# A state space stage in a hybrid decoder: response matrices loaded without their zero corner, first ones at the end of the MLP before it, and its small products one weight tile later

## The chip, the cores and the metric

The kernel runs on one core of one Trainium2 chip. The metric is the device time of one execution in microseconds (us). "TensorE" is PE in the profile, "VectorE" DVE, "ScalarE" ACT, "GpSimd" POOL and "SyncE" SP; SP and POOL are the two engines that issue the DMAs named below.

## What is computed

Two layers over 256 tokens of width 2048, each a token mixer, a cross-attention to 256 memory tokens and a squared-ReLU MLP of width 8192, with RMSNorm before each and residual adds. The mixer of layer 0 is a chunked gMLP, that of layer 1 the state space layer that the change touches:

```python
def s5_glu(h, w_in, lam_re, lam_im, log_dt, bm_re, bm_im, cm_re, cm_im, d_skip, w_out, b_out):
    u = (h @ w_in).astype(F32).reshape(bsz, seq, B_GROUPS, B_GROUP)     # 128 groups of 16 channels
    lam_bar = jnp.exp(lam * dt)                                         # 64 complex states per group
    b_bar = ((lam_bar - 1.0) / lam)[..., None] * bmat
    bu = jnp.einsum('gpc,bsgc->sbgp', b_bar, u.astype(jnp.complex64))
    _, states = lax.associative_scan(combine, (a, bu), axis=0)          # s_t = lam_bar * s_(t-1) + bu_t
    y = jnp.einsum('gcp,sbgp->bsgc', cmat, states).real + d_skip.astype(F32) * u
    y = jax.nn.gelu(y.reshape(bsz, seq, B_WIDTH), approximate=False).astype(h.dtype)
    val, gate = jnp.split(y @ w_out + b_out, 2, axis=-1)
    return val * jax.nn.sigmoid(gate)
```

Everything is fp32 in and out.

## The kernel before

**Weights.** A weight matrix is read in tiles of 128x1024 fp32 (512 KB). `wload` (L123) issues a tile's DMA on SP into `wraw` (4 buffers); `wtile` has ACT cast it to its high part `whi` (L102) and DVE subtract that to get the low part `wlo` (L103), 3 buffers each. A product is three matmuls, whi with the activations' high part, wlo with their high part, whi with their low part, so a tile is 12 matmuls of 128x512. In the state space stage they stand at L154, in the MLP at L171/L173 (up) and L801 to L803 (down).

**Order of the work.** After each weight tile's matmuls the program calls `tick()`. A tick runs what `at(delay, fn)` planned for it, and in the first MLP every second tick takes one step from the list `side`. So delays count weight tiles, and each engine's instruction order is fixed by when the program writes them, except that a side step is written with a priority of 200 instructions later. `issue_after(self.fed)` holds a DMA on SP behind the last weight load written so far.

**Side steps in the first MLP (`ssm_prep`, 680 to 1320 us).** The matrices that the state space stage needs are worked out beside the first MLP's matmuls and stored to DRAM: `Pd` (inputs to states), `Qd` (states to outputs) and `Kd` (the response of 8 positions to their own inputs, a band of 15x16 values per group and channel). For each of 32 quads of groups there are three steps: `quad` loads (`lb<-in_b_pc` and `lb<-Ld`, L1047), `quad_q` makes `Qd` and `Kd` (matrix products at L1085, stores at L1081 and L1093), `quad_p` makes `Pd` (DVE L1103 to L1106, store L1107).

**The state space stage (`s5`).** `gemm_tok` multiplies by `b_w_in` in four column chunks n of 8 tiles each. After chunk n, `chunks(n)` scales and reorders the result into `u` (DVE L1161, ACT L1164), and `follow(n)` plans the small products by weight tiles: `inputs` (8 transposes of `u` on PE, L1175) at 3, `own` (products with `pq`, L1189) at 4, `states` (transposes L1205, copies to `vv` on ACT L1209, whose first column is zeroed by POOL, L1200) at 5, `carry` (the scan, four DVE operations L1221 to L1224 each) at 6 to 9, `outputs` (products with `dq` L1237 and `qq` L1243) in two halves at 13 and 15, `features` (gelu on ACT L1250, transposes on PE L1255, split into high and low part on ACT L102 and DVE L103) at 17. `dq` is read from the band in `Kd` as full 128x1024 matrices: of the band of 8 positions to 8, what lies ahead of the diagonal is zeros that `quad_q` stored.

**Loads of the small matrices.** `pq`, `dq` and `qq` have 4 buffers each and 4 loads of 512 KB per chunk. For chunk 0, `pq` is issued on POOL as soon as the last store is done, `dq` on SP among the weight loads (ticks 2, 6, 10, 14), and `qq` on POOL at ticks 6 and 8 after chunk 0. For chunks 1 to 3 all three go through POOL, `pq` at 4, `dq` and `qq` at 6 and 8.

**The GLU.** `b_w_out` follows in the same way. Its first three accumulators are fed by k-ranges so that late features are needed late: k-tiles 0 to 7 three times, then 8 to 11 three times, a `flush()` of the plan, and 12 to 15. Chunk n's features are k-tiles 4n to 4n+3.

Of the kernel before, what the change touches and what calls it, by code (L numbers as in the profile page):

```python
# [16 lines left out]
P = 128  # L17
# [21 lines left out]
class Trunk:  # L39
# [854 lines left out]
    def ssm_prep(self, pool):  # L894
# [220 lines left out]
        for q in range(G // 4):  # L1115
            sd += [lambda q=q: quad(q), lambda q=q: quad_q(q), lambda q=q: quad_p(q)]


    def s5(self, x, cur, nxt):
# [3 lines left out]
        with tc.tile_pool(name="s5", bufs=2, reuse_waits="tile") as sp:  # L1123
# [5 lines left out]
            def load(src, nm, shape, stream):  # L1129
                t = sp.tile(shape, F32, name=nm, bufs={"pq": 4, "dq": 4, "qq": 4}[nm])  # L1130
                if stream:
                    with tc.issue_after(self.fed):
                        nc.sync.dma_start(out=t, in_=src)
                else:
                    nc.gpsimd.dma_start(out=t, in_=src)
                return t

            def fetch(nm, n, i, stream=False):

                if nm == "pq":  # L1140
                    t = load(self.Pd[4 * n + i], nm, [P, 2, 4, P], stream)
                elif nm == "qq":
                    t = load(self.Qd[4 * n + i].rearrange("l p r n -> (l p) r n"), nm, [P, 2, 4 * P], stream)
                else:
                    kd = self.Kd[4 * n + i]
                    t = load(bass.AP(tensor=kd.tensor, offset=kd.offset,
                                     ap=[[P, T], [(2 * T - 1) * P, 16], [1, T * P]]), nm, [P, T * P], stream)
                ahead[nm, n, i] = t
# [46 lines left out]
            def states(n):  # L1195
# [4 lines left out]
                nc.gpsimd.memset(vv[:, :, 0, :], 0.0)  # L1200
# [45 lines left out]
            def features(n):  # L1246
                py = st.pop(n)[2]
                y = sp.tile([P, T, 4, 2, 16], F32, name="y", tag="z", bufs=1)
                for l in range(2):
                    nc.scalar.activation(out=y[:, :, :, l, :].rearrange("p j i c -> p i j c"),  # L1250
                                         in_=py[l].rearrange("p i (j c) -> p i j c", j=T), func=AF.Gelu)
                for h in range(2):
# [7 lines left out]
            def follow(n):  # L1260

                for i in range(4):
                    if n + 1 < NCH:
                        self.at(4, lambda i=i: fetch("pq", n + 1, i))
                    if n:
                        self.at(6 + i // 2 * 2, lambda i=i: fetch("dq", n, i))
                    self.at(6 + i // 2 * 2, lambda i=i: fetch("qq", n, i))
                self.at(3, lambda: inputs(n))
                self.at(4, lambda: own(n))
                self.at(5, lambda: states(n))  # L1270
                self.at(6, lambda: [carry(n, 2, 15), carry(n, 4, 7, 2)])
                self.at(7, lambda: [carry(n, c, 1, 4) for c in (8, 12, 16)])
                self.at(8, lambda: [carry(n, c, 1, 4) for c in (20, 24, 28)])
                self.at(9, lambda: [carry(n, 6, 7, 2), carry(n, 3, 15)])
                self.at(13, lambda: outputs(n, 0))
                self.at(15, lambda: outputs(n, 1))
                self.at(17, lambda: features(n))

            for i in range(4):
                fetch("pq", 0, i)  # L1280
                self.at(4 * i + 2, lambda i=i: fetch("dq", 0, i, True))
# [9 lines left out]
            for j in range(NCH):  # L1291
                if j == 0:
# [4 lines left out]
                    av, ag, _ = (part(n, acc, (0, 8)) for n, acc in ((0, None), (NCH, None), (1, av1)))  # L1297
                    for n, acc in ((0, av), (NCH, ag), (1, av1)):
                        part(n, acc, (8, 12))
# [210 lines left out]
```

## Time and profile before

| | us |
|---|---|
| median of 3 runs | 2824.2 |
| the runs | 2821.84, 2825.02, 2824.2 |
| the profiled execution's own time | 2824.95 |
| its span, first to last instruction | 2823.2 |
| outside the span | 1.75 |

The profiled execution stands 0.75 us above the median. In the profile each engine has its own row of work; a row of the waits names the engine that sat idle, the operation it sat before, and the operation whose end released it. PEclk is the granted TensorE clock as a share of full speed; its two levels are 1.2 and 2.4 GHz.

### The profile page before, as it was taken

Reading aid. Unit: us, or ns where it says so; the run is one execution under the profiler, and the core shown is the slowest. Engines: PE = TensorE matmul, PEld = TensorE weight load, DVE = VectorE, ACT = ScalarE, POOL = GpSimd, SP = SyncE. Lnnn points to the kernel's source line nnn. Section 1 sums busy time; section 2 is a strip of 40 time slices with the busy share of each in tenths; the row PEclk is TensorE's granted clock in tenths of the full one; section 3 lists DMA queues with packets and bytes.
Section 4 is the critical chain, followed back from the end, with each engine's and each line's share of the span. In section 5 each row is a group of like instructions: output and inputs, shape, how many; then the busy total and the mean of one; then the engine's idle time right before and its main releaser. Section 6 shows DMA issues by size and latency. Waiting matters only on the chain.

```text
span 2823.2 us, 39558 instructions
## 1 busy us (share of the span) xinstructions
PE 2781.1 (99%) x15020; PEld 2329.6 (83%) x15020; DVE 1993.0 (71%) x2743; ACT 1399.7 (50%) x1801; POOL 202.6 (7%) x378
## 2 busy tenths in 40 slices
PE   9999999999999999999989999999999999999998
PEld 7888888888888888888867888888888888888886
DVE  6755756788878878786557667557777767667665
ACT  6445545555434444344445445445554545445444
POOL 0100000001022222221001000000000000000000
PEclk9999999999999999999999999999999999999999
DMA  8767655548688888887679777564556566565655
GB/s 289 231 205 217 209 179 172 180 148 262 196 270 260 249 257 262 249 262 234 189 237 284 220 214 224 177 195 152 182 160 215 171 216 194 163 217 166 218 177 157
DMA packets 189615, 596.85 MB, mean 211 GB/s; under 512 B 37632, under 2 KB 39856, under 8 KB 188912
## 3 DMA queue, kind: packets, MB, share of 16 engines
q1 hardware_dynamic: 151936, 532.22, 60.6%
q0 software_dynamic: 37344, 62.04, 8.1%
q8 instruction: 117, 1.92, 0.3%
q14 instruction: 74, 0.61, 0.1%
q10 hardware_dynamic: 144, 0.07, 0.0%
HBM read 570.66 MB, written 23.46 MB: 210 GB/s over the span
## 4 chain that ended last, share of the span: by engine, by line
PE 88%; DVE 4%; issue 3%; DMA 2%; ACT 2%; POOL 0%; ACTq 0%; SPq 0%; POOLq 0%; DVEq 0%
PE acc L171 23%; PE acc L718 21%; PE acc L154 13%; PE acc L173 12%; PE acc L801 4%; PE acc L803 4%; PE acc L802 4%; DVE wlo L103 1%; DMA wraw<-in_b_w_in 1%; PE ps L503 1%; ACT whi L102 1%; PE ps L581 1%; PE ps L154 1%; PE ps L222 1%; ACT u L1164 0%
## 5 line engine op out<-in xcount | busy, mean ns | idle before, releaser
L103 DVE TENSOR_TENSOR wlo<-wraw,whi 128x1024 fp32r<-128x1024 f32 x892 | 1090.6, 1224 | 662.4 <-ACT whi L102 658.0
L102 ACT CAST whi<-wraw 128x1024 fp32r<-128x1024 f32 x892 | 938.2, 1053 | 1154.2 <-PE acc L171 385.1
L171 PE MATMUL acc<-act,whi 128*128 128x512 f32 x3072 | 1084.4, 397 | 0.0
L173 PE MATMUL acc<-act,wlo 128*128 128x256 f32 x3072 | 863.1, 281 | 1.2 <-DVE wlo L103 1.2
L171 PEld LDWEIGHTS acc<-act,whi 128*128 128x128 f32 x3072 | 576.5, 188 | 139.7 <-issue 3.4
L173 PEld LDWEIGHTS acc<-act,wlo 128*128 128x128 f32 x3072 | 580.3, 189 | 2.7 <-DVE wlo L103 2.0
L154 PE MATMUL acc<-whi,act 128*128 128x512 f32 x1472 | 464.6, 394 | 15.8 <-ACT whi L102 14.1
L154 PEld LDWEIGHTS acc<-whi,act 128*128 128x128 f32 x1472 | 278.2, 189 | 75.8 <-ACT whi L102 14.5
L154 PE MATMUL acc<-wlo,act 128*128 128x512 f32 x736 | 287.9, 392 | 4.0 <-DVE wlo L103 4.0
L718 PE MATMUL acc<-whi,act 128*128 128x512 f32 x864 | 273.6, 390 | 1.2 <-DVE ends L560 1.0
L802 PE MATMUL acc<-wlo,hh 128*128 128x512 f32 x544 | 212.1, 390 | 3.2 <-DVE wlo L103 3.2
L801 PE MATMUL acc<-whi,hh 128*128 128x512 f32 x544 | 213.5, 392 | 0.0
L803 PE MATMUL acc<-whi,hl 128*128 128x512 f32 x544 | 212.6, 391 | 0.0
L718 PEld LDWEIGHTS acc<-whi,act 128*128 128x128 f32 x864 | 162.0, 188 | 37.6 <-ACT whi L102 2.6
L718 PE MATMUL acc<-wlo,act 128*128 128x512 f32 x432 | 168.7, 390 | 0.0
L154 PEld LDWEIGHTS acc<-wlo,act 128*128 128x128 f32 x736 | 138.7, 188 | 33.3 <-DVE wlo L103 5.3
L718 PE MATMUL acc<-whi,hh 128*128 128x512 f32 x378 | 147.6, 394 | 0.5
L718 PE MATMUL acc<-wlo,hh 128*128 128x512 f32 x378 | 147.2, 389 | 0.0
L718 PE MATMUL acc<-whi,hl 128*128 128x512 f32 x378 | 146.1, 389 | 0.0
L802 PEld LDWEIGHTS acc<-wlo,hh 128*128 128x128 f32 x544 | 102.1, 188 | 24.4 <-DVE wlo L103 3.5
L801 PEld LDWEIGHTS acc<-whi,hh 128*128 128x128 f32 x544 | 102.1, 188 | 22.8 <-issue 2.0
L803 PEld LDWEIGHTS acc<-whi,hl 128*128 128x128 f32 x544 | 102.1, 188 | 22.3 <-issue 1.0
(364 smaller groups left out, 2674.0 us busy)
## 6 DMA issues: line engine op xcount, KB each, us to landing
wraw<-in_f_w_up SPq DMA_DIRECT2D x256, 512.0 KB, 4.4
wraw<-in_f_w_down SPq DMA_DIRECT2D x228, 512.0 KB, 4.3
wraw<-in_a_w_in SPq DMA_DIRECT2D x64, 512.0 KB, 4.7
wraw<-in_x_w_q SPq DMA_DIRECT2D x64, 512.0 KB, 3.7
wraw<-in_x_w_k SPq DMA_DIRECT2D x64, 512.0 KB, 3.6
wraw<-in_b_w_out SPq DMA_DIRECT2D x64, 512.0 KB, 4.6
wraw<-in_x_w_v SPq DMA_DIRECT2D x48, 512.0 KB, 4.4
wraw<-in_x_w_o SPq DMA_DIRECT2D x48, 512.0 KB, 4.1
```

Of the source, the lines that this page charges most:

```text
L102: self.nc.scalar.copy(out=hi, in_=src)
L103: return self.nc.vector.tensor_tensor(out=lo, in0=src, in1=hi.bitcast(F32), op=ALU.subtract).ins
L154: nc.tensor.matmul(out[t], pairs[m][0][:, kt, sl], pairs[m][1][:, kk, :], start=st and m == 0, stop=en and m == 2)
L171: nc.tensor.matmul(acc[:, f, :], hi[:, kk, sl], both[:, kt].rearrange("p a s -> p (a s)"), start=st, stop=False, skip_group_check=True)
L173: nc.tensor.matmul(acc[:, f, 0:S], lo[:, kk, sl], ah[:, kt, :], start=False, stop=en, skip_group_check=True)
L222: nc.tensor.transpose(pt[:, kk, t * P:(t + 1) * P], src[:, t, c:c + P], self.ident)
L503: mm = lambda s, m, b, e: nc.tensor.matmul(sc[:, t, :], s, m, start=b, stop=e, skip_group_check=True)
L581: mm = lambda s, mv, b, e: nc.tensor.matmul(op[:, k, :], s, mv, start=b, stop=e, skip_group_check=True)
L718: mm = lambda s, m, e: nc.tensor.matmul(out, s, m, start=key not in begun, stop=e, skip_group_check=True)
L801: nc.tensor.matmul(acc[:, t, :], ah[:, kt % 4, sl], hi[:, kk, :], start=st, stop=False)
L802: nc.tensor.matmul(acc[:, t, :], ah[:, kt % 4, sl], lo[:, kk, :], start=False, stop=False)
L803: nc.tensor.matmul(acc[:, t, :], al[:, kt % 4, sl], hi[:, kk, :], start=False, stop=en)
```

## The change

- In `ssm_prep` two empty side steps stand between the first `quad_q` and the first `quad_p`; all later side steps come 4 ticks later.
- The response matrices live in four fixed tiles whose zero corner is written once (12 memsets on POOL). Each is then loaded by four DMAs of 32 partitions, of 256, 512, 768 and 1024 values per partition, 320 KB together, in place of one of 512 KB.
- Chunk 0's `dq` are issued on POOL right behind its `pq`; chunk 0's `qq` on SP at ticks 2, 4, 6, 8.
- The zeroing of `vv`'s first column moves from POOL to DVE.
- In `follow` everything is one tile later (`own` is written ahead of the fetches of that tile), and `features` is cut in two: the gelu (`activated`) right after the second half of `outputs`, transposes and split at 19 for chunks 0 and 1, at 17 for chunks 2 and 3.
- The GLU's first parts are cut finer: k-tiles 0 to 3, 4 to 7 and 8 to 11, three accumulators each.

```diff
--- before.py
+++ after.py
@@ -1113,7 +1113,10 @@
         sd += [lambda k=k: power(k) for k in range(5, T + 1)]
         sd += [lambda: spread(5), lambda: (last(), inputs(0))]
         for q in range(G // 4):
-            sd += [lambda q=q: quad(q), lambda q=q: quad_q(q), lambda q=q: quad_p(q)]
+            sd += [lambda q=q: quad(q), lambda q=q: quad_q(q)]
+            if q == 0:
+                sd += [lambda: None] * 2
+            sd += [lambda q=q: quad_p(q)]
 
 
     def s5(self, x, cur, nxt):
@@ -1126,25 +1129,33 @@
 
             ahead = {}
 
-            def load(src, nm, shape, stream):
-                t = sp.tile(shape, F32, name=nm, bufs={"pq": 4, "dq": 4, "qq": 4}[nm])
+            def load(src, out, stream=False):
                 if stream:
                     with tc.issue_after(self.fed):
-                        nc.sync.dma_start(out=t, in_=src)
+                        nc.sync.dma_start(out=out, in_=src)
                 else:
-                    nc.gpsimd.dma_start(out=t, in_=src)
-                return t
+                    nc.gpsimd.dma_start(out=out, in_=src)
+
+            resp = [sp.tile([P, T * P], F32, name=f"dq{i}", bufs=1) for i in range(4)]
+            for t in resp:
+                for h in range(3):
+                    nc.gpsimd.memset(t[0:96 - 32 * h, 2 * h * P:2 * (h + 1) * P], 0.0)
 
             def fetch(nm, n, i, stream=False):
 
+
                 if nm == "pq":
-                    t = load(self.Pd[4 * n + i], nm, [P, 2, 4, P], stream)
+                    t = sp.tile([P, 2, 4, P], F32, name=nm, bufs=4)
+                    load(self.Pd[4 * n + i], t, stream)
                 elif nm == "qq":
-                    t = load(self.Qd[4 * n + i].rearrange("l p r n -> (l p) r n"), nm, [P, 2, 4 * P], stream)
+                    t = sp.tile([P, 2, 4 * P], F32, name=nm, bufs=4)
+                    load(self.Qd[4 * n + i].rearrange("l p r n -> (l p) r n"), t, stream)
                 else:
-                    kd = self.Kd[4 * n + i]
-                    t = load(bass.AP(tensor=kd.tensor, offset=kd.offset,
-                                     ap=[[P, T], [(2 * T - 1) * P, 16], [1, T * P]]), nm, [P, T * P], stream)
+                    t, kd = resp[i], self.Kd[4 * n + i]
+                    for h in range(4):
+                        load(bass.AP(tensor=kd.tensor, offset=kd.offset + 6 * P,
+                                     ap=[[P, 2], [(2 * T - 1) * P, 16], [1, 2 * (h + 1) * P]]),
+                             t[32 * h:32 * h + 32, 2 * (3 - h) * P:])
                 ahead[nm, n, i] = t
 
             def chunks(n, acc):
@@ -1197,7 +1208,7 @@
                 z = st[n].pop()
                 vv = sp.tile([P, 2, NC, NQ // 2], F32, name="vv")
                 st[n] += [vv]
-                nc.gpsimd.memset(vv[:, :, 0, :], 0.0)
+                nc.vector.memset(vv[:, :, 0, :], 0.0)
                 for h in range(2):
                     pt = self.ps([P, 2, 2, 4, NC])
                     for i in range(2):
@@ -1243,12 +1254,15 @@
                                 nc.tensor.matmul(py[l][32 * t:32 * t + 32, i, :], vv[s, r, :, 4 * t + i],
                                                  qv[s, r, t], start=False, stop=(r == 1), skip_group_check=True)
 
-            def features(n):
+            def activated(n):
                 py = st.pop(n)[2]
-                y = sp.tile([P, T, 4, 2, 16], F32, name="y", tag="z", bufs=1)
+                y = st[n] = sp.tile([P, T, 4, 2, 16], F32, name="y", tag="z", bufs=1)
                 for l in range(2):
                     nc.scalar.activation(out=y[:, :, :, l, :].rearrange("p j i c -> p i j c"),
                                          in_=py[l].rearrange("p i (j c) -> p i j c", j=T), func=AF.Gelu)
+
+            def features(n):
+                y = st.pop(n)
                 for h in range(2):
                     pt = self.ps([P, 4, 4, NC])
                     for i in range(4):
@@ -1259,26 +1273,29 @@
 
             def follow(n):
 
+                self.at(5, lambda: own(n))
                 for i in range(4):
                     if n + 1 < NCH:
-                        self.at(4, lambda i=i: fetch("pq", n + 1, i))
+                        self.at(5, lambda i=i: fetch("pq", n + 1, i))
                     if n:
-                        self.at(6 + i // 2 * 2, lambda i=i: fetch("dq", n, i))
-                    self.at(6 + i // 2 * 2, lambda i=i: fetch("qq", n, i))
-                self.at(3, lambda: inputs(n))
-                self.at(4, lambda: own(n))
-                self.at(5, lambda: states(n))
-                self.at(6, lambda: [carry(n, 2, 15), carry(n, 4, 7, 2)])
-                self.at(7, lambda: [carry(n, c, 1, 4) for c in (8, 12, 16)])
-                self.at(8, lambda: [carry(n, c, 1, 4) for c in (20, 24, 28)])
-                self.at(9, lambda: [carry(n, 6, 7, 2), carry(n, 3, 15)])
-                self.at(13, lambda: outputs(n, 0))
-                self.at(15, lambda: outputs(n, 1))
-                self.at(17, lambda: features(n))
+                        self.at(7 + i // 2 * 2, lambda i=i: fetch("dq", n, i))
+                        self.at(7 + i // 2 * 2, lambda i=i: fetch("qq", n, i))
+                self.at(4, lambda: inputs(n))
+                self.at(6, lambda: states(n))
+                self.at(7, lambda: [carry(n, 2, 15), carry(n, 4, 7, 2)])
+                self.at(8, lambda: [carry(n, c, 1, 4) for c in (8, 12, 16)])
+                self.at(9, lambda: [carry(n, c, 1, 4) for c in (20, 24, 28)])
+                self.at(10, lambda: [carry(n, 6, 7, 2), carry(n, 3, 15)])
+                self.at(14, lambda: outputs(n, 0))
+                self.at(16, lambda: outputs(n, 1))
+                self.at(16, lambda: activated(n))
+                self.at(17 if n >= NCH - 2 else 19, lambda: features(n))
 
             for i in range(4):
                 fetch("pq", 0, i)
-                self.at(4 * i + 2, lambda i=i: fetch("dq", 0, i, True))
+            for i in range(4):
+                fetch("dq", 0, i)
+                self.at(2 * i + 2, lambda i=i: fetch("qq", 0, i, True))
             for n in range(NCH):
                 acc = self.gemm_tok(hT, a["b_w_in"], n)
                 if n == 0:
@@ -1294,9 +1311,10 @@
                     av1 = [spare.tile([P, NB], F32, name="ps") for _ in range(2)]
                     part = lambda n, acc, k: self.gemm_tok(yT, wo, n, acc=acc, kts=range(*k), first=k[0] == 0,
                                                            last=k[1] == KT)
-                    av, ag, _ = (part(n, acc, (0, 8)) for n, acc in ((0, None), (NCH, None), (1, av1)))
-                    for n, acc in ((0, av), (NCH, ag), (1, av1)):
-                        part(n, acc, (8, 12))
+                    av, ag, _ = (part(n, acc, (0, 4)) for n, acc in ((0, None), (NCH, None), (1, av1)))
+                    for k in (4, 8):
+                        for n, acc in ((0, av), (NCH, ag), (1, av1)):
+                            part(n, acc, (k, k + 4))
                     self.flush()
                     for n, acc in ((0, av), (NCH, ag)):
                         part(n, acc, (12, KT))

```

How the order on the engines changes, at three places.

DVE in the first MLP, its first down-projection tiles (`wlo` low half of a weight tile, `hl` low part of the hidden activations, `po` the first operation of the first `quad_p`, which reads `lb`; `bcq`, `TC`, `qt` belong to `quad_q` and the powers). Before, from the first hidden part to the second:

```order
L103 TENSOR_TENSOR wlo<-wraw,whi 128x1024
L103 TENSOR_TENSOR hl<-r,hh 128x512
L1103 TENSOR_TENSOR po<-lb 128x512
L103 TENSOR_TENSOR wlo<-wraw,whi 128x1024 x2
L1055 TENSOR_SCALAR bcq<-bcq,sg 128x128
L103 TENSOR_TENSOR wlo<-wraw,whi 128x1024
L177 TENSOR_TENSOR r<-acc,r 128x512
L634 SCALAR_TENSOR_TENSOR r<-r 128x512
L103 TENSOR_TENSOR wlo<-wraw,whi 128x1024
L103 TENSOR_TENSOR hl<-r,hh 128x512
```

Now, from the weight tile ahead of the same second hidden part on:

```order
L103 TENSOR_TENSOR wlo<-wraw,whi 128x1024
L103 TENSOR_TENSOR hl<-r,hh 128x512
L1027 TENSOR_TENSOR TC_5679<-TC_5679 128x64
L1072 TENSOR_TENSOR qt<-T_5684,bcq 128x4x9x16
L1023 TENSOR_SCALAR TC_5680<-TC_5680 128x64
L1073 TENSOR_TENSOR tq<-T_5685,bcq 128x576
L1026 TENSOR_TENSOR TC_5680<-TC_5680 128x64
L1074 TENSOR_TENSOR qt<-qt,tq 128x4x9x16
L103 TENSOR_TENSOR wlo<-wraw,whi 128x1024
L1028 TENSOR_TENSOR TC_5679<-TC_5679,TC_5680 128x64
L1103 TENSOR_TENSOR po<-lb 128x512
```

`po` stood right behind the first `hl`, ahead of five low halves; it now stands behind them and the second `hl`.

SP, from the last MLP weights on (`Kd` and `Qd` are the sources of `dq` and `qq`). Before:

```order
L123 DMA wraw<-in_b_w_in 128x1024 x6
L1133 DMA dq<-Kd_5662 128x1x1024
L1133 DMA dq<-Kd_5663 128x1x1024
L123 DMA wraw<-in_b_w_in 128x1024 x4
L1133 DMA dq<-Kd_5664 128x1x1024
L123 DMA wraw<-in_b_w_in 128x1024 x4
L1133 DMA dq<-Kd_5665 128x1x1024
```

Now:

```order
L123 DMA wraw<-in_b_w_in 128x1024 x6
L1135 DMA qq<-Qd_5646 128x1024
L1135 DMA qq<-Qd_5647 128x1024
L1135 DMA qq<-Qd_5648 128x1024
L123 DMA wraw<-in_b_w_in 128x1024 x2
L1135 DMA qq<-Qd_5649 128x1024
L123 DMA wraw<-in_b_w_in 128x1024 x24
```

The four `dq` loads are gone from SP, and the four `qq` loads stand in their place, three of them ahead of the seventh tile.

POOL, from the last store of the side steps on. Before:

```order
L1093 DMA Kd_5677<-kd 240x1x16 x8
L1135 DMA pq<-Pd_5630 128x1024
L1135 DMA pq<-Pd_5631 128x1024
L1135 DMA pq<-Pd_5632 128x1024
L1135 DMA pq<-Pd_5633 128x1024
L1200 MEMSET vv 128x2x16
L1135 DMA qq<-Qd_5646 128x1024
L1135 DMA qq<-Qd_5647 128x1024
L1135 DMA qq<-Qd_5648 128x1024
L1135 DMA qq<-Qd_5649 128x1024
L1200 MEMSET vv 128x2x16
L112 DMA bc<-in_b_b_out 128x512 x2
```

Now, from the last tile's memsets on:

```order
L1142 MEMSET dq_12619 96x256
L1142 MEMSET dq_12619 64x256
L1142 MEMSET dq_12619 32x256
L1137 DMA pq<-Pd_5630 128x1024
L1137 DMA pq<-Pd_5631 128x1024
L1137 DMA pq<-Pd_5632 128x1024
L1137 DMA pq<-Pd_5633 128x1024
L1137 DMA dq_12616<-Kd_5662 32x1x256
L1137 DMA dq_12616<-Kd_5662 32x1x512
L1137 DMA dq_12616<-Kd_5662 32x1x768
L1137 DMA dq_12616<-Kd_5662 32x1x1024
L1137 DMA dq_12617<-Kd_5663 32x1x256
```

The `qq` loads stood behind a memset of `vv`; now the loads of chunk 0 that POOL issues stand behind the memsets of the corner alone.

## Rows read from the trace of the kernel before

**Rows 1.** The page's part 1: busy time (share of the span) xinstructions.
```profile
PE 2781.1 (99%) x15020; PEld 2329.6 (83%) x15020; DVE 1993.0 (71%) x2743; ACT 1399.7 (50%) x1801; POOL 202.6 (7%) x378
```

**Rows 2.** Waits of PE, 1400 to 1700 us: us in total, times, longest.
```profile
PE acc L154 <- ACT whi L102: 7.2, 1, 7.2
PE ps L1175 <- ACT u L1164: 4.4, 4, 1.7
PE acc L154 <- DVE wlo L103: 2.3, 2, 1.8
PE acc L154 <- ACT act L102: 1.5, 1, 1.5
...
PE acc L154 <- DVE act L103: 0.3, 1, 0.3
```

**Rows 3.** Waits of PE, 400 to 800 us.
```profile
PE acc L802 <- DVE wlo L103: 3.2, 1, 3.2
```

**Rows 4.** Timeline of DVE, then PE, near 757 us: start, duration, [idle before <-releaser].
```profile
757.26 0.69 DVE L1103 TENSOR_TENSOR po<-lb 128x512 f32<-128x512 f32 x1 [5.75 <-DMA lb<-Ld]
757.87 2.35 DVE L103 TENSOR_TENSOR wlo<-wraw,whi 128x1024 fp32r<-128x1024 f32 x2
...
759.14 0.50 PE L802 MATMUL acc<-wlo,hh 128*128 128x512 f32 x1 [3.18 <-DVE wlo L103]
```

**Rows 5.** Timelines of POOL and SP, the MLP's end.
```profile
1400.40 0.12 POOL L1200 MEMSET vv<- 128x32 f32 x1 [77.19 <-PE acc L802]
1400.64 2.10 POOL L1135 DMA_DIRECT2D qq<-Qd  x4
...
1400.73 1.48 SPq L1133 DMA_DIRECT2D dq<-Kd  x2
1403.18 9.19 SPq L123 DMA_DIRECT2D wraw<-in_b_w_in  x4
```

**Rows 6.** Timelines of ACT and PE, the seventh tile.
```profile
1423.92 1.04 ACT L102 CAST whi<-wraw 128x1024 fp32r<-128x1024 f32 x1 [13.17 <-DMA wraw<-in_b_w_in]
...
1425.02 0.80 PE L154 MATMUL acc<-whi,act 128*128 128x512 f32 x1 [7.20 <-ACT whi L102]
```

**Rows 7.** Windows: busy (x) by engine, PEclk, DMA share, GB/s.
```profile
1320.00:1332.00 12.00, 12.00 (x55) 9.94 (x54) 5.90 (x5) 4.35 (x5) 3.21 (x6) 1.00 0.88 334
1400.40:1420.00 19.60, 17.42 (x81) 14.11 (x79) 9.89 (x25) 7.02 (x12) 3.41 (x8) 1.00 0.99 244
1423.10:1429.80 6.70, 4.32 (x9) 3.09 (x10) 3.67 (x3) 3.13 (x3) 0.00 (x0) 0.50 0.73 206
1473.20:1541.00 67.80, 63.27 (x746) 48.95 (x747) 52.97 (x121) 39.23 (x76) 13.74 (x26) 1.00 1.00 282
```

**Rows 8.** Timeline of PE, transposes of the first chunk's inputs.
```profile
1445.66 1.09 PE L1175 MATMUL ps<-ident,u 128*128 128x128 f32 x8 [1.74 <-ACT u L1164]
```

**Rows 9.** Timeline of DVE, before the late low half at 1504.9 us.
```profile
1503.65 2.36 DVE L103 TENSOR_TENSOR wlo<-wraw,whi 128x1024 fp32r<-128x1024 f32 x2
```

**Rows 10.** Timeline of POOL: first response load of chunks 1 and 3.
```profile
1480.50 0.62 POOL L1135 DMA_DIRECT2D dq<-Kd  x1 [2.75 <-PE ps L1237]
...
1552.81 0.61 POOL L1135 DMA_DIRECT2D dq<-Kd  x1 [25.85 <-PE ps L1237]
```

**Rows 11.** Timeline of PE: first uses in chunks 1 and 3, last in 3.
```profile
1515.28 0.64 PE L1237 MATMUL ps<-dq,us 128*32 128x128 f32 x16
...
1578.84 0.65 PE L1237 MATMUL ps<-dq,us 128*32 128x128 f32 x16
...
1588.10 0.64 PE L1237 MATMUL ps<-dq,us 128*32 128x128 f32 x16
```

**Rows 12.** The page's part 6: KB each, median us to landing.
```profile
dq<-Kd POOLq DMA_DIRECT2D x12, 512.0 KB, 16.5
...
bcq<-in_b_bc POOLq DMA_DIRECT2D x32, 128.0 KB, 4.9
...
Kd<-kd POOLq DMA_DIRECT2D x128, 15.0 KB, 4.5
```

## The prediction

> **What bounds the kernel now.** I read the page's first part, then PE's waits by stretch, then the timelines around the long ones. PE is busy for 2781.1 of 2823.2 us [rows 1], so the kernel is a stream of matmuls, and apart from the matmuls themselves only PE's waits can be won. The table of PE's waits for the state space stage [rows 2] shows the whole of what the change can reach there: 7.2 us for one cast, 4.4 us in four waits for `u`, 2.3 us in two waits for a low half (1.8 and 0.5), 1.5 and 0.3 us for split features. In the first MLP there is one wait worth a row, 3.2 us for a low half [rows 3]. The matmuls are not fewer after the change, only in another order, so the sum below is made of waits, and of one stretch of slow clock that a wait leaves behind.
>
> The 3.2 us: DVE sat before `po` (L1103) for 5.75 us until `lb` landed; the low half queued behind it came late, and PE's L802 waited [rows 4].
>
> The 7.2 us: when the MLP's last matmul ended at 1400.4, POOL's memset of `vv`, which had waited 77 us for it, let go four `qq` loads, 2 MB, and SP issued two `dq` loads, 1 MB, at 1400.73. The weight loads from the seventh tile on were issued behind them, from 1403.18 [rows 5]. ACT then sat 13.17 us until that tile landed, and PE's first matmul with it began at 1425.02 after a wait of 7.20 [rows 6]. The DMA engines were busy for 0.99 of that stretch and moved only 244 GB/s, against 334 at a share of 0.88 in the stretch where the `pq` loads run [rows 7].
>
> The clock: behind this wait the granted clock was 0.50, the level of 1.2 GHz, for 6.7 us in which PE was busy 4.32 us [rows 7]. At the full level that work takes half, so 2.2 us went there.
>
> **The change part by part.**
>
> *Two empty side steps.* `po` of the first quad now stands behind five more low halves and the second `hl`. A tile takes 12 matmuls, about 2.7 us, so DVE, which came to it at 751.5 (757.26 less 5.75), comes to it some 11 us later, near 762, when `lb`, which landed at 757.26 [rows 4], is there. All later steps come four ticks later too, and the stage has them done around 1320, 80 us ahead of their first use. Gain 3.2. Bounds: 0 if another load is late in its place, 3.2 if none.
>
> *Chunk 0's loads.* `dq` leaves SP and is issued behind `pq` near 1325, in a stretch where PE worked without a gap beside four 512 KB loads, busy for 12.00 us of 12.00 [rows 7]. `vv`'s memset leaves POOL. What stands ahead of the seventh tile is then three `qq`, 1.5 MB, where 3 MB stood. It was issued at 1403.18; PE was free at 1417.82, and the cast takes 1.1, so it may land up to 1416.7, 13.5 us after its issue. It took some 20.6 (ACT's cast began at 1423.92). In proportion to the bytes ahead and its own, 2 MB in place of 3.5, it takes 11.8; one `qq` is issued before the MLP's end, so sooner. Margin 1.7 or more. Gains: 7.2, the 0.5 behind it, and 2.2 of clock: 9.9. Bounds: 0 and 9.9; I take all of it.
>
> *The small products one tile later.* `inputs` waited four times for ACT's `u`, 1.74 at the first [rows 2, 8]. A tile's delay is 2.7 us, more than any of these waits, but ACT and DVE must serve one more tile's cast and low half before, 1.05 and 1.2 us, so about 1.6 of a wait is covered. I keep 0.4 in all and take a gain of 4.0. Bounds: 2 to 4.4.
>
> *DVE's blocks.* The 1.8 us low half came behind two `u` pieces and the last carry, queued ahead of it on DVE [rows 2, 9]. With `inputs` and the carries a tile later the carries no longer share their tile with the same `u` pieces. Gain 1.8, but DVE is busy for 53.0 of 67.8 us there [rows 7], so I count 1.0 of new small waits against all of this part. Bounds: 1.8 gained to 1.8 lost at each of three places.
>
> *Features and the GLU's parts.* `features(1)` used to end one tick before its first use as k-tile 4. With parts of four k-tiles its first use is at tick 39, and it is planned for 35. The gelu runs earlier than the transposes, so PE does not stand behind it. The waits of 1.5 and 0.3 go [rows 2]: gain 1.7. Chunk 3's transposes stay at tick 49, with a gelu one tile ahead of them.
>
> *The cut response loads.* Bytes per chunk fall from 4 MB to 3.3, but `dq` is now 16 loads and not 4. No row shows a load of 32 partitions. The nearest: a whole one took 16.5 us in this crowded stretch, a 128 KB load 4.9 and a 15 KB store 4.5 elsewhere [rows 12]. Chunk 3 has the least room: its first `dq` was issued at 1552.81 and used at 1578.84, 26.0 us later [rows 10, 11]. Even 16.5 is less. Cost 0, as long as loads run side by side; when they do not is a rival.
>
> *No cost.* 12 memsets on POOL, which is busy for 7% of the span [rows 1] and writes these 80 us ahead of use. `vv`'s memset on DVE is one operation per chunk, four of some 0.2 us, inside the 1.0 above.
>
> Sum: 3.2 + 9.9 + 4.0 + 1.8 + 1.7 = 20.6, less 1.0: 19.6. The profiled execution took 2824.95 with 1.75 outside its span, and stands 0.75 above the median of 2824.2. So 2805.3 from the one and 2804.6 from the other: **2805**.
>
> **The rivals.**
>
> *The burst stays.* The change only trades 1 MB of `dq` for 1.5 MB of `qq` ahead of the same weight load on the same queue, and two of those still wait for room that the MLP gives up at its end. If the seventh tile lands more than 13.5 us after its issue, PE waits as now; if all of it stays, the change does not do what its second part says, and the time is 2805 + 9.9 = 2815. For: 244 GB/s at a full share [rows 7]. Against: 2 MB of `qq` no longer start with it.
>
> *DVE becomes the bound.* Three more waits like the 1.8, one in each later chunk: 2805 + 5.4 = 2810. For: DVE's 78% there. Against: the stretch between chunks has few waits now.
>
> *The cut loads are late, and it is slower.* Ten loads are issued per half chunk. The compiled program has POOL's DMAs count on eight semaphores in turn, so each waits for the eighth before it. If a piece takes as long as a whole one did, 16.5 us, the first half's last loads land 2 x 16.5 = 33 us after the first issue, and the second half's 3 x 16.5 = 49.5. Chunk 3 has 26.0, and 35.3 to its last use [rows 10, 11]: 7.0 late, then 49.5 - 35.3 - 7.0 = 7.2 more. Chunk 1 had 34.8 us (1480.50 to 1515.28) and, by the same 9.3 between first and last use, 44.1: 5.4 late, and chunk 2 is taken alike. Together 25, so 2805 + 25 = 2830. It decides where a piece lands later than about 12 to 13 us. Against: eight pieces in flight hold some 1.3 MB (3.3 MB over 20 loads, times 8), where up to 4 MB were in flight, and if time goes with the bytes in flight a piece takes about 16.5 x 1.3 / 4 = 5.4 us.
> The Trainium skill speaks against the cut: its page "DMA: Bandwidth & Descriptors", section Bandwidth, wants DMAs batched to a MiB and calls transfers under 64 KB bound by their descriptors, and its section on the anatomy of one DMA gives 2.0 us and the bytes over 436 GB/s; the four pieces one after another would by an estimate from it take 8.8 us where the whole one takes 3.2, 35 us per chunk. The trace disagrees on the whole load, which took 16.5 us and not 3.2; of pieces no run here shows it yet.
>
> *Nothing to be seen.* The waits move to other operations of PE's queue and come back one by one: 2824.
>
> **How the numbers follow.** A change of 0.2%, 5.6 us, is about what a measurement of this kernel tells from none. The sum as told: 0.80 (2801 to 2809). The burst stays: 0.06 (2815). DVE: 0.06 (2810). Late pieces: 0.04 (2830). Nothing: 0.04 (2824). The first three are faster by over 5.6 us, 0.92; same 0.04; slower 0.04. The range: with every wait of [rows 2, 3] and the 2.2 of clock gone, 21.1 us from the median, 2803, and the runs reach 2.4 below their median: 2800. At the top it takes in DVE's case and the staying burst: 2815. The last two, 0.08, are left out, and the sum's own tails.
>
> **What would show it.** PE's waits in the state space stage under 2 us in all, none at L802 in the first MLP; `po` starting without a wait for `lb`; the seventh weight tile's DMA landing before 1417 less 3 us, counted on the shorter time line; PEclk 1.00 through the change from MLP to state space stage; POOL waiting for no DMA of its own before L1237 needs it. I would be wrong if PE shows waits for a DMA of `dq` or `qq` at L1237 or L1243, or if the wait for `whi` at the seventh tile is still there, or if new waits for `wlo` sum to over 5 us.

## The result, and the profile after

| | before | changed |
|---|---|---|
| median of 6 runs each, us | 2821.28 | 2806.51 |
| lowest and highest | 2818.26, 2825.02 | 2803.91, 2808.84 |
| profiled execution's span | 2823.2 | 2806.7 |

The ratio is 0.9946, with a 95% interval of 0.9934 to 0.9958: faster by 14.8 us by the medians (12 to 19 by the interval). The forecast was 2805, in a range of 2800 to 2815, and 19.6 us of gain. That the time came within 1.5 us of the forecast is partly luck: three more runs of the kernel before lowered its median by 2.9. The gain was 4.8 us smaller than forecast, and that difference is the subject of what follows.

PE's waits in the state space stage of the changed kernel, 1400 to 1700 us (in total, times, longest), against [rows 2]:

```profile
PE acc L154 <- ACT u L1175: 2.9, 1, 2.9
PE ps L1248 <- issue: 1.1, 1, 1.1
PE ps L1186 <- ACT u L1175: 0.9, 1, 0.9
PE ps L1248 <- ACT vv L1220: 0.3, 1, 0.3
```

All rows of [rows 2] are gone but part of the one for `u`: 16.0 us of waits (15.7 in the rows shown there and 0.3 for `vv`) became 5.2. The largest row, for an accumulator, is new, and so is the 1.1 at the response matrices (L1248 is L1237 of before).

Windows of the changed kernel: the passage from MLP to state space stage, and the 6.7 us behind the new wait (us, busy by engine with instructions, PEclk, DMA share, GB/s), against [rows 7]:

```profile
1395.00:1440.00 45.00, 45.00 (x267) 37.27 (x266) 27.00 (x47) 27.36 (x49) 2.10 (x4) 1.00 0.77 254
...
1516.90:1523.60 6.70, 6.60 (x17) 5.21 (x18) 4.82 (x8) 2.71 (x5) 4.76 (x8) 0.54 0.89 250
```

PE has no gap and full clock where it lost 9.9 us. In the second window it has work for 6.60 us at a granted clock of 0.54: some 3.0 us (6.60 x 0.46) are lost to the clock there, more than the 2.2 that the old wait left.

SP at the end of the first MLP, ACT's cast of the seventh tile, and the landing of the weight loads issued from 1396 to 1420:

```profile
1395.00 1.46 SPq L1135 DMA_DIRECT2D qq<-Qd  x3
1397.27 3.81 SPq L123 DMA_DIRECT2D wraw<-in_b_w_in  x2
```
```profile
1406.52 1.05 ACT L102 CAST whi<-wraw 128x1024 fp32r<-128x1024 f32 x1 [1.67 <-PE acc L154]
```
```profile
DMA to landing us min/median/max: 4.2/4.4/4.4
```

The seventh tile stands behind three `qq` loads as the order said. The trace holds no landing for it and for the eighth. But its cast, which was held by PE and not by a DMA, began at 1406.52, so it landed within 9.3 us of its issue at 1397.27, sooner than the 11.8 that the proportion of bytes had given. The loads issued from 1403.58 on landed in 4.2 to 4.4 us: no burst is left to see.

DVE in the first MLP, the first `po`:

```profile
759.74 0.68 DVE L103 TENSOR_TENSOR hl<-r,hh 128x512 fp32r<-128x512 f32 x1
...
764.66 0.68 DVE L1103 TENSOR_TENSOR po<-lb 128x512 f32<-128x512 f32 x1
```

It no longer waits [rows 4], and PE has no wait left in the first MLP's down-projection.

### The profile page after: what moved, and what is told of

Its sections match the earlier page's. It is cut to its first block, busy times and chain, and to the rows that moved or that the text cites. A ratio compares the mean times of both kernels' runs of the same rounds, so it can differ in the third digit from the quotient of the medians.

```text
span 2806.7 us, 39629 instructions
## 1 busy us (share of the span) xinstructions
PE 2778.8 (99%) x15020; PEld 2330.8 (83%) x15020; DVE 1993.0 (71%) x2747; ACT 1400.0 (50%) x1801; POOL 233.1 (8%) x434
```

## The experiments

Each was timed beside runs of the kernel before on the same chip (medians of before 2820.1 to 2821.3), so ratios compare better than times. The source lines of a run can be a few lower or higher than those of the changed kernel: L1175 of before, L1181 and L1186 are all the transposes of `u`.

**The loads alone.** The kernel before with

```diff
-                nc.gpsimd.memset(vv[:, :, 0, :], 0.0)
+                nc.vector.memset(vv[:, :, 0, :], 0.0)
...
-                    self.at(6 + i // 2 * 2, lambda i=i: fetch("qq", n, i))
+                        self.at(6 + i // 2 * 2, lambda i=i: fetch("qq", n, i))
...
-                self.at(4 * i + 2, lambda i=i: fetch("dq", 0, i, True))
+            for i in range(4):
+                fetch("dq", 0, i)
+                self.at(2 * i + 2, lambda i=i: fetch("qq", 0, i, True))
```

> The kernel before with one part of the change: chunk 0's dq issued on POOL behind its pq, chunk 0's qq on SP at ticks 2, 4, 6, 8, and vv's memset on DVE; dq stays whole (512 KB), all delays as before. My theory: the wait of 7.2 us for the seventh weight tile, the 0.5 behind it and the stretch at half clock go, 9.9 us together: about 2811 against 2821 before, ratio 0.9965; the four waits of PE for u stay (4.4 us). Rival 1: three qq ahead of the seventh tile delay it as the dq did, ratio 0.999 or more. Rival 2: the burst's end also ends part of the waits for u, since the ninth and tenth tiles came late too, ratio 0.995.

Measured 2813.3, ratio 0.9972 (0.9962 to 0.9982), 7.9 us faster by the ratio (5 to 11) and 6.8 by the medians. PE's largest waits from 1380 to 1640 us:

```profile
PE ps L1175 <- ACT u L1164: 2.6, 3, 1.7
PE acc L154 <- DVE wlo L103: 1.8, 1, 1.8
PE acc L154 <- ACT act L102: 1.4, 1, 1.4
```

The 7.2 and the 0.5 are gone, and the rest of [rows 2] stands but for 1.8 us of the waits for `u`, most of it in the first (1.7 before, 0.2 here). About half of the change's gain is this part, with `dq` still whole: rival 1 falls. The 1.8 us look like rival 2, but the next run has the first of these waits at 0.2 too, with the burst's wait still at 6.4 us, so that the burst made it is not shown.

**The empty side steps alone.**

```diff
-            sd += [lambda q=q: quad(q), lambda q=q: quad_q(q), lambda q=q: quad_p(q)]
+            sd += [lambda q=q: quad(q), lambda q=q: quad_q(q)]
+            if q == 0:
+                sd += [lambda: None] * 2
+            sd += [lambda q=q: quad_p(q)]
```

> The kernel before with the two empty side steps alone. My theory: DVE's wait for lb at L1103 (5.75 us) and PE's wait of 3.2 us at L802 go, nothing comes for them: 3.2 us less, ratio 0.9989. Rival: another load of the shifted side steps is late in its place, or the low halves wait behind another block: ratio 1.000, with a wait of PE in 750 to 800 us.

Measured 2818.7, ratio 0.9993 (0.9984 to 1.0001). PE has no wait from 700 to 1380 us in its profile, where 3.4 us stood; the time went down 1.7, which the interval does not tell from none. The mechanism is seen, its price on the median is not. Its row for the first wait for `u`:

```profile
1437.96 1.09 PE L1178 MATMUL ps<-ident,u 128*128 128x128 f32 x8 [0.19 <-ACT u L1167]
```

**Everything one tile earlier.** The changed kernel with `follow`'s old delays (`inputs` at 3 to `outputs` at 13 and 15, gelu at 15):

```diff
-                self.at(4, lambda: inputs(n))
-                self.at(6, lambda: states(n))
+                self.at(3, lambda: inputs(n))
+                self.at(4, lambda: own(n))
+                self.at(5, lambda: states(n))
```

> The changed kernel with follow's delays as before (inputs at 3 and so on, own after the fetches), gelu right behind the second half of outputs at 15, transposes of the features still at 19 and 17. My theory: the waits for u come back, 3 to 4 us, and PE's new wait of 2.9 us near 1514 us with the half clock behind it (about 3 us) goes if the later carries caused it: 2804 to 2806, ratio 0.994. Rival: the new wait comes from the moved features or the GLU's parts and stays, and the waits for u come on top: 2810, ratio 0.996.

Measured 2811.9, ratio 0.9964 (0.9951 to 0.9978). PE's largest waits, 1380 to 1640 us, and the row of the second:

```profile
PE ps L1186 <- ACT u L1175: 4.0, 3, 2.1
PE ps L154 <- ACT whi L102: 2.7, 1, 2.7
```

```profile
1522.28 1.22 PE L154 MATMUL ps<-whi,act 128*128 128x512 f32 x2 [2.70 <-ACT whi L102]
```

The waits for `u` are back, 4.0 for 0.9. A wait of nearly the same size stands near the GLU's start, but it is not the same one: on PE the third weight tile there goes to the accumulator of n = 1 (`ps`) and not to the gate's, and PE waits for the tile's cast, which ACT ran between pieces of `u`. The time is nearer to the rival's; whether the later delays made the wait of 2.9 this run leaves open, and the next ones settle it.

**Features and the GLU's parts undone.** The changed kernel with `features` at 17 for all chunks, and the first parts as before:

```diff
-                self.at(17 if n >= NCH - 2 else 19, lambda: features(n))
+                self.at(17, lambda: features(n))
...
-                    av, ag, _ = (part(n, acc, (0, 4)) for n, acc in ((0, None), (NCH, None), (1, av1)))
-                    for k in (4, 8):
-                        for n, acc in ((0, av), (NCH, ag), (1, av1)):
-                            part(n, acc, (k, k + 4))
+                    av, ag, _ = (part(n, acc, (0, 8)) for n, acc in ((0, None), (NCH, None), (1, av1)))
+                    for n, acc in ((0, av), (NCH, ag), (1, av1)):
+                        part(n, acc, (8, 12))
```

> The changed kernel with the transposes of all chunks' features at 17 and the GLU's first parts as before (k-tiles 0 to 7, then 8 to 11). My theory: the features of chunk 1 come one tick ahead of their first use again, waits of 1.5 and 0.3 us come back, the new wait of 2.9 us near 1514 us stays since the carries cause it: 2808, ratio 0.9952. Rival: that wait goes with the features' move, 5 to 6 us less: 2802, ratio 0.993.

Measured 2803.8, ratio 0.9939 (0.9926 to 0.9951). The first three of PE's five waits, 1380 to 1640 us:

```profile
PE ps L1186 <- ACT u L1175: 0.9, 1, 0.9
PE acc L154 <- ACT act L102: 0.7, 1, 0.7
PE acc L154 <- DVE act L103: 0.6, 1, 0.6
```

The 2.9 us are gone with the later delays still in place, and the small waits for split features are back: the rival holds, and by the profile this part of the change gave nothing. By the times it cannot be said, since the interval overlaps that of the change.

**Which half of it.** Two runs took it apart. `room` (below) keeps both halves and the wait of 2.9 us, and `room_features_17` takes `features` back to 17 with the finer parts kept:

> As room, and the transposes of all chunks' features at 17, with the GLU's finer parts kept. My theory: the wait of 2.9 us near 1514 us and the half clock behind it go, since ACT's u for chunk 3 no longer shares its ticks with the split of chunk 1's features; and the waits for split features (1.3 us in features_17) do not come, since chunk 1's features are first used at tick 39: PE's waits in 1380 to 1640 us under 2 us, 2799 to 2801, ratio 0.9925. Rival: the finer parts themselves keep the wait: 2804.

Measured 2806.0, ratio 0.9951 (0.9938 to 0.9963), and in its profile:

```profile
PE acc L154 <- ACT u L1170: 3.5, 1, 3.5
```

The wait stays: my theory falls, the finer parts make it. ACT and PE of the changed kernel show how:

```profile
1513.20 1.23 ACT L1175 ACTIVATE u<-acc,rstd 32x128 f32<-32x128 f32 x4 [1.91 <-DVE u L1172]
1514.46 1.05 ACT L102 CAST whi<-wraw 128x1024 fp32r<-128x1024 f32 x1
1515.71 1.24 ACT L1175 ACTIVATE u<-acc,rstd 32x128 f32<-32x128 f32 x4 [0.20 <-DVE u L1172]
```
```profile
1517.00 0.80 PE L154 MATMUL acc<-whi,act 128*128 128x512 f32 x1 [2.86 <-ACT u L1175]
```

PE starts 0.05 us after the last `u` that reads the accumulator of `b_w_in`'s last chunk (1515.71 + 1.24). `psA` has two accumulators. With parts of eight k-tiles the gate's accumulator (`ag`, the second) begins at the GLU's fifth weight tile; with parts of four at its third, when ACT and DVE still read the buffer. The next run only changes the order, so that `ag` begins at the fifth tile again:

```diff
-                    av, ag, _ = (part(n, acc, (0, 4)) for n, acc in ((0, None), (NCH, None), (1, av1)))
+                    av, _, ag = (part(n, acc, (0, 4)) for n, acc in ((0, None), (1, av1), (NCH, None)))
                     for k in (4, 8):
-                        for n, acc in ((0, av), (NCH, ag), (1, av1)):
+                        for n, acc in ((0, av), (1, av1), (NCH, ag)):
```

> The changed kernel with the GLU's finer parts taken in another order: the two accumulators n = 0 and n = 1 first, the gate's third, so that the gate's accumulator begins at the fifth weight tile of the GLU again and not at the third. My theory: it takes the PSUM buffer that the last chunk of b_w_in still holds until ACT and DVE have made u of it; the wait of 2.9 us near 1514 us (PE, acc, released by ACT u) and the half clock behind it (3 us) go: 2801, ratio 0.9925. Rival: ACT's casts are late there for any order, the wait stays with another tile's name (ps in place of acc), 2806.

Measured 2805.4, ratio 0.9947 (0.9936 to 0.9959), the median no better than the change's. Its profile:

```profile
PE ps L1186 <- DVE act L103: 1.8, 1, 1.8
PE ps L1248 <- issue: 1.4, 1, 1.4
```
```profile
1510.00:1520.00 10.00, 10.00 (x49) 8.15 (x48) 9.45 (x36) 7.46 (x19) 6.56 (x11) 1.00 0.81 238
```

The wait for the accumulator and the half clock are gone as expected, and 1.8 us for a buffer of the transposes came, where chunk 1's features are split late. The mechanism is shown; that it is worth several us is not.

**The room of the memory loads.** The changed kernel had one more wait outside the stage, in the next attention. Rows of POOL, DVE and PE of the changed kernel:

```profile
1714.81 1.06 POOL L284 DMA_DIRECT2D memc<-in_mem_t  x2 [47.93 <-issue]
...
1734.80 1.14 DVE L288 TENSOR_SCALAR memc<-memc,gcol 128x256 f32<-128x256 f32 x4 [2.24 <-DMA memc<-in_mem_t]
...
1737.13 0.38 PE L173 MATMUL acc<-act,wlo 128*128 128x256 f32 x1 [1.14 <-DVE wlo L103]
```

Two such waits, 2.3 us, stand there. Before there was one of 1.0, and the loads were issued right behind POOL's last bias load:

```profile
1684.37 1.06 POOL L284 DMA_DIRECT2D memc<-in_mem_t  x2
```

My reading of the program: the fixed tiles are requested ahead of the first `pq`, so they took the places that `pq` had, and `pq` (with `val` and `gat`, which share its buffers) those of `dq`; `memc`'s buffers lie there too, and the GLU's last `val` and `gat` free them late. The profile names no releaser for the 47.93 us, but the last read of `val` (DVE, L1342) ended at 1714.26, 0.55 us before the load. The edit puts the places back:

```diff
-            resp = [sp.tile([P, T * P], F32, name=f"dq{i}", bufs=1) for i in range(4)]
...
             for i in range(4):
                 fetch("pq", 0, i)
+            resp = [sp.tile([P, T * P], F32, name=f"dq{i}", bufs=1) for i in range(4)]
...
```

> The changed kernel with the four fixed tiles for dq set up after chunk 0's pq loads instead of before them, so that dq and pq lie in the places that they had before. My theory: in the changed kernel the next attention's memory loads (memc) took the room of val and gat, which the GLU's last column gives up late, and were issued at 1714.8 us, 48 us after POOL was free; with dq and pq in their old places they are issued right after the last bias load again, and PE's two waits at L173 near 1737 us (2.3 us) fall to under 1: 1.3 to 2 us under the changed kernel, ratio 0.994. The wait of 2.9 us near 1514 us stays. Rival: these waits come from the DMA queue's load there and stay at 2 us or more.

Measured 2804.7, ratio 0.9940 (0.9928 to 0.9953). POOL, and PE's waits from 1640 us on:

```profile
1666.91 1.07 POOL L284 DMA_DIRECT2D memc<-in_mem_t  x2
```
```profile
PE acc L173 <- DVE wlo L103: 0.5, 1, 0.5
```

The load is 48 us earlier, and the waits are 1.8 us less, as expected. The median is 1.8 us lower too, which the intervals do not tell from none.

**The cut loads.** POOL in the changed kernel, chunk 0's loads, and the page's part 6:

```profile
1334.07 2.23 POOL L1137 DMA_DIRECT2D pq<-Pd  x4
1336.22 2.50 POOL L1137 DMA_DIRECT2D dq<-Kd  x4
1340.13 0.59 POOL L1137 DMA_DIRECT2D dq<-Kd  x1 [1.41 <-DMA pq<-Pd]
```
```profile
qq<-Qd POOLq DMA_DIRECT2D x12, 512.0 KB, 10.5
...
dq<-Kd POOLq DMA_DIRECT2D x16, 128.0 KB, 9.8
...
dq<-Kd POOLq DMA_DIRECT2D x16, 32.0 KB, 10.8
```

The ninth load waits for the first, as the third rival said. POOL waited 43 us in all for its own DMAs before `dq` loads (21.3 for `pq`, 13.0 for `dq`, 9.0 for `qq`). A piece of 32 KB took as long as one of 128, or as a `qq` of 512.

PE's new wait of 1.1 us at L1248 is not one for a late piece. In the changed kernel, then in `room_ag_later_whole` (below), which loads the matrices whole:

```profile
1496.36 0.43 PE L1248 MATMUL ps<-dq,us 128*32 128x128 f32 x8
1497.88 0.43 PE L1248 MATMUL ps<-dq,us 128*32 128x128 f32 x8 [1.09 <-issue]
```
```profile
1496.12 0.63 PE L1241 MATMUL ps<-dq,us 128*32 128x128 f32 x12
1497.62 0.41 PE L1241 MATMUL ps<-dq,us 128*32 128x128 f32 x4 [0.88 <-issue]
```

It stands in the middle of the 16 matmuls of one `dq` tile, the first of which had read all 128 partitions; the profile names no releaser ("issue"); and with whole loads it is there as well (0.9, and 0.4 in `whole_dq`). Its cause is open.

Three runs changed the cut. In `whole_dq` the changed kernel loads each matrix whole into the fixed tiles; `room_ag_later_whole` does so on `room_ag_later`, and `room_two_pieces` loads two pieces of 64 partitions on `room_features_17`. The edit of the first:

```diff
-                    for h in range(4):
-                        load(bass.AP(tensor=kd.tensor, offset=kd.offset + 6 * P,
-                                     ap=[[P, 2], [(2 * T - 1) * P, 16], [1, 2 * (h + 1) * P]]),
-                             t[32 * h:32 * h + 32, 2 * (3 - h) * P:])
+                    load(bass.AP(tensor=kd.tensor, offset=kd.offset,
+                                 ap=[[P, T], [(2 * T - 1) * P, 16], [1, T * P]]), t, stream)
```

> The changed kernel with each response matrix loaded by one DMA of 512 KB into the same four fixed tiles, its zero corner loaded too, no corner memsets. My theory: cutting the loads gains nothing; POOL's waits for its own DMAs (43 us in the changed kernel) go, PE's wait of 1.1 us at L1248 goes, time 0 to 1.5 us under the changed kernel, ratio to before 0.994. Rival: the 0.77 MB less per chunk matters, the whole loads take 16 us again and pq or dq come late, 2 to 5 us above the changed kernel, ratio 0.996.

> As room_features_17, with each response matrix loaded in two DMAs of 64 partitions (128 and 256 KB) and not four, one memset per tile. My theory: POOL's DMAs wait for the one eight before, so with 12 loads per chunk in place of 20 POOL's waits for its own DMAs fall from over 40 us to under 15, and PE has no wait at L1248 beyond 0.3; time 0 to 1 us under room_features_17, ratio 0.992. Rival: bytes count more (384 KB for 320 KB per matrix) and landing times rise above 12 us with no gain.

> As room_ag_later, with each response matrix loaded whole by one DMA of 512 KB. My theory: no wait of PE in this stage hangs on these loads, so it is within 2 us of room_ag_later, and the cut of the loads is worth nothing by itself. Rival: the cut saves bytes when the DMA engines are full, and the whole loads are slower by 3 us or more, as whole_dq stood 4 us above the changed kernel in the medians, with waits at L1243 or L1249 or later weight tiles to show for it.

| | us | ratio to before | landing of dq, median us |
|---|---|---|---|
| the change (four pieces) | 2806.5 | 0.9946 (0.9934 to 0.9958) | 10.3 |
| whole_dq | 2810.6 | 0.9960 (0.9948 to 0.9973) | 20.3 |
| room_features_17 (four) | 2806.0 | 0.9951 (0.9938 to 0.9963) | 9.3 |
| room_two_pieces | 2806.3 | 0.9948 (0.9934 to 0.9961) | 15.4 |
| room_ag_later (four) | 2802.7 | 0.9939 (0.9927 to 0.9951) | 10.1 |
| room_ag_later_whole | 2804.5 | 0.9950 (0.9937 to 0.9962) | 20.5 |

Two pieces are no different from four in time; POOL's waits for its own DMAs before `dq` loads fell to 22 us, not under 15, and the landing rose, as that run's rival said. Whole loads took these waits down to 4.7 us in `whole_dq`, and still stood 3 to 4 us slower both times by the ratios (by the medians of the same rounds the second pair differs by 1.8, within my theory's 2). But the intervals overlap, and no profile shows where the time would go: that of `whole_dq` has PE waits of 5.5 us in the stage against 5.2, and it is of its fastest execution (2806.7, the others 2809.6 to 2811.1). That the cut saves time is not shown.

**The two edits together.** Fixed tiles after the first `pq` and the gate's accumulator third, then also `features` at 17:

> Both: fixed tiles set up after chunk 0's pq loads (as room) and the gate's accumulator third (as ag_later). My theory: PE's waits in the state space stage fall to under 2 us and those of the next attention to under 1, the two gains add: about 2799, ratio 0.9925 or less, faster than both kernels shown. Rival: what one saves the other meets again later, 2803.

> As room_ag_later, with the transposes of all chunks' features at 17. My theory: the wait of 1.8 us for a buffer of the transposes that the split of chunk 1's features gives up late (L1181, released by DVE's act) goes, since that split comes two tiles earlier, and with the gate's accumulator third the 3.5 us of room_features_17 do not come: PE's waits in the state space stage under 2 us, 2800 to 2803, ratio 0.993 to 0.994, no slower than room_ag_later. Rival: the earlier split meets u of chunk 3 on ACT and DVE and a wait of 2 us or more comes back there, 2804 to 2806.

Measured 2802.7, ratio 0.9939 (0.9927 to 0.9951), and 2801.8, ratio 0.9932 (0.9918 to 0.9945). For the first, the waits in the stage are 3.0 us and not under 2, and the time is the rival's. The second is 19.6 us under the kernel before in its own rounds (2821.3), and some 5 under the change by the medians; their intervals overlap, so that it is faster than the change is not shown. PE's waits of the last one, 1380 to 1640 us:

```profile
PE ps L154 <- DVE wlo L103: 1.2, 1, 1.2
PE ps L1181 <- ACT u L1170: 0.9, 1, 0.9
PE ps L1243 <- ACT vv L1215: 0.7, 1, 0.7
PE ps L1264 <- ACT y L1256: 0.4, 1, 0.4
```

3.2 us in four, none followed by slow clock, where I had expected under 2.

## Why the prediction was right, and where it was not

*The empty side steps*, gain 3.2: the wait is gone in the changed kernel and with the steps alone.

*Chunk 0's loads*, gain 9.9: the waits and the slow clock are gone, and this part alone gave 7.9 us (5 to 11). The seventh tile's landing was estimated by bytes at 11.8 us; it took 9.3 at most, so the estimate was on the safe side.

*One tile later*, gain 4.0: 3.5 by the waits (4.4 to 0.9), and 4.0 stand there again with the old delays. The first of the four waits, 1.7 before, is at 0.2 in all three runs that keep the old delays, so that part of the 3.5 need not be the later tile's.

*DVE's blocks*, gain 1.8: the row is gone.

*Features and the GLU's parts*, gain 1.7: **this is the step that failed.** The waits of 1.5 and 0.3 went, as the step says, but it looked at the inputs of the finer parts alone and not at the accumulators that they take. The gate's accumulator was asked for two tiles earlier, 2.9 us before it was free, and in the profiled execution 3.0 us of slow clock followed: 1.7 gained became 4.2 lost. The 1.0 "of new small waits" had no such thing in it.

*The cut response loads*, cost 0: no wait of PE for a piece is in the profile; the 1.1 us at L1248 were not in the sum, and whole loads have such a wait too. A piece was estimated to take 5.4 us by the bytes in flight; it took 9 to 11, near the 12 to 13 at which the third rival would have begun to decide. That rival did not come, but its mechanism, the ninth load behind the first, is in the trace.

*Not in the working at all*: the fixed tiles moved other buffers, and the next attention's memory loads came 48 us later; 2.3 us of waits where 1.0 stood.

By these rows, each of one execution, the sum is 20.6 - 0.5 - 2.9 - 3.0 - 1.1 - 1.3 = 11.8, of 14.8 (12 to 19) measured. Of the profiled spans' difference of 16.5 us, 1.4 lies in a wait for a low half in the gMLP, which the change does not touch (1.7 before, 0.3 after, and from none to 1.8 in other runs); the rest lies in PE's busy time and was not traced further.

The range held since its lower terms were bounded by what the waits could give. Neither the burst nor DVE came as a rival. Of the signs that the prediction named, two failed: the waits of the stage came to 5.2 us and not under 2, and POOL did wait for its own DMAs.

## What to carry to other kernels

When work is cut into finer parts, list for each part not only the data that it needs but the buffer that it takes, and who still reads that buffer at its new time. When a tile is requested earlier in a program, look at who inherits its place, as far as into the next stage. A small wait for PE can cost twice its length if the clock falls behind it, as 2.9 us did here with 3.0 of slow clock, and another of 3.2 us cost no more than itself: look at the granted clock behind each wait before ranking them.

## What the runs showed of the hardware that was not expected

Landing times of `dq` loads on POOL's queue were about 10 us in four pieces, 15.4 in two, 20 to 21 whole, but hardly differed by size within a run: for the pieces of 32 KB and those of 128 KB the medians were 10.8 and 9.8. The `qq` loads between them, 512 KB in every run, rose in the same way: 10.5 us in the changed kernel, 17.0 in `room_two_pieces`, 21.7 in `whole_dq`. That is as if the bytes of all loads in flight set the time of each, which no run tested by itself; the `pq` loads, issued apart from these, did not rise (10.1, 9.2, 8.2). The estimate that the prediction drew from the Trainium skill ("DMA: Bandwidth & Descriptors", the section on the anatomy of one DMA), 2.0 us and the bytes over 436 GB/s, is under all of these, 2.1 to 3.2; no run here has a load alone on the queue.

The clock: behind the wait of 2.9 us the granted clock was 0.54 over the next 6.7 us. Behind the wait of 3.2 us in the first MLP of the kernel before it stayed at 1.00, as this window shows:

```profile
759.10:766.00 6.90, 6.86 (x34) 5.50 (x35) 6.39 (x9) 4.67 (x10) 0.00 (x0) 1.00 0.75 246
```

Behind the wait of 2.1 us for `u` in `follow_early` it was 0.75 over the next 6.8. And the same wait for the gate's accumulator, 2.9 us in `room` and 3.5 in `room_features_17`, was followed by 0.77 and 0.75 over 6.7 us, as the second of them shows here:

```profile
1521.40:1528.10 6.70, 6.66 (x22) 5.42 (x23) 4.68 (x7) 2.09 (x2) 2.89 (x5) 0.75 1.00 260
```

So waits of the same length, even at the same place, differ in what follows them, and the 3.0 us of slow clock behind the change's wait are those of its profiled execution; in these two runs it was about half. What tells them apart was not tried.
